# A two-layer hybrid attention backbone: queries and gates projected with features on partitions, and reciprocal sums spread through DRAM

## The chip, the cores and the metric

The kernel runs on one core of one Trainium2 chip. The metric is the device time of one execution in microseconds; the median of three runs before the change is 1154.01 us (1152.91 to 1156.14). All arithmetic is in fp32; where TensorE is to run at its faster fp32r rate, each operand is split into a high part (rounded to fp32r) and a low part (the rest), and a product is made of three matmuls: high x high, high x low, low x high.

## What is computed

Two layers work on 512 latent tokens and 256 context tokens of width 1024. In each layer a modulated RMSNorm feeds one input projection of 4608 columns. These are split among three groups of eight heads (head width 64) and a gate of 1536 columns. Cut to what the change touches:

```python
# A: global attention, q and k normalised per head, rotary on latent tokens
q = apply_rope(rmsnorm(heads(q, 8), qn), cos, sin) * HEAD_DIM ** -0.5
p = softmax(q @ k_all.T);  ya = p @ v_all              # k_all: 512 latent + 256 context keys
# B: 16-column neighbourhood of the 8 x 64 grid, with a learned bias, plus context keys
# C: window of +-128 tokens with a sink logit, rotary, plus context keys
ux = concat([ya, yb, yc]) * silu(px[9])                # the gate
x = x + gate * (ux @ w_out)
```

Context tokens go through the same weights in layer 0 as queries that read context keys alone. In layer 1 only latent queries are needed. So a layer has 6 tiles of 128 query tokens (layer 0) or 4 (layer 1), called `nq`.

## The kernel before

**Stages.** A prologue (L370 to L447) norms x, makes the modulation and accumulates the first projections while it goes. Then `mixers` runs once for each layer, and after each an output projection (L530 on) makes the residual and the next layer's norm, or the result. Inside `mixers` the heads go in pairs: 4 pairs of B, 4 of A, 4 of C, twelve to a layer, in the order of `PLAN` (L34). While pair n attends, the projections of pair n+1 are made: `weave` (L1406) alternates the two generators by their costs. Only the first slot of a layer has no attention in it.

**Two ways to project.** `proj_f` (L295) puts 128 output features on partitions and tokens in columns: the weights are stationary, and the moving operand has 512 latent or 256 context columns. `proj_t` (L316) puts 128 tokens on partitions: the normed activations are stationary and 256 columns of weights move. Either accumulates 24 matmuls (8 slices of the 1024 inputs, three products each) in a PSUM bank and then calls `done`, which empties the bank. Steady banks are `pj` (two), `T` (two, for transposes), `Sbig` (three, scores) and `Obig` (one, head outputs in two halves).

- B's q and k and all of C (with its gates) come from `proj_f`.
- A's k and v, B's v, **A's q with A's gate** (`a_pair`, L863), and **B's gates** (`b_g`, L923) come from `proj_t`.

**A's q before** (`a_pair`, `rope_a`). For each two tiles of tokens, with a head's 64 features side by side in the free dimension, the rotation, the sum of squares and the normalisation run on POOL (pair 0 on DVE), the result is split in high and low, and four fp32r transposes (L879) bring the features to partitions; ACT copies them to Q. The scale of 1/8 and the norm weight lie in the tables made by `tables_a`.

**C's q** (`rope_c`, `c_q`) has features on partitions from the start. ACT copies the bank to `tA`; four DMAs on SP's queue swap quarters of 32 partitions (L958); three POOL operations rotate (L959 to L961); ACT and POOL write the high and low parts (L969, L970).

**Attention.** For each head `scores` puts q k into `Sbig`; DVE takes the negated maximum, ACT the exponential with its sum; SP's DMA moves P to fp32r tiles (`ship`, L1030). `values` turns P by fp32r transposes into T (L1044), ACT and DVE split it (`pt_copy`: `pth` L778, `ptl` L1024), and matmuls with v accumulate in Obig. `o_out` (L1060) adds its halves into the pair's tile `OT`, features on partitions. There is one `OT` and one `u` buffer.

**Finish of a pair** (`finish`, L1314). The reciprocals of the sums are `rec`: 128 tokens by 2 heads by `nq`. They are needed along columns, so POOL multiplies each tile of the gate (A, B) or of ones (C) by its reciprocal (L1339), an fp32 transpose turns each tile (L1347, recorded at L1047), and DVE multiplies OT by it (L1350, L1357). For C, whose gate has features on partitions, POOL multiplies by the gate after that (L1353, L1355). The product `u` is stored to DRAM on ACT's queue (L1365), or, for the last three in `FT_ORDER`, split at once for the output projection. C's last pair of a layer uses `end=True`: one DVE copy spreads the reciprocals (L1335), and DVE does the gate.

**The order.** `arrange` (L1918) sorts all instructions before the program is built. It knows a cost for each kind (`Step.cost`, L1609; for a DMA issue, transfer and landing), the buffers each tag has (`CAPS`) and the dependencies, runs a list scheduler six times with ranks from a backward pass, and fixes the best order of each engine. Engines then run these queues in order.

## Time and profile before

| what | value |
|---|---|
| median of three runs | 1154.01 us (1152.91 to 1156.14) |
| the profiled execution | 1156.11 us, span 1154.3 us |
| TensorE busy, instructions | 1122.4 us (97%), 8016 |
| DVE, ACT, POOL busy | 763.6, 685.9, 405.9 us |
| mean granted TensorE clock | 0.997 |
| DMA | 191.40 MB, 105760 packets |

A row of the timeline is: start, length, engine, line, operation, output and inputs, partitions x elements, and a count where like rows are merged. A matmul's length holds its way through the array, so one begins before the last has ended; the distance of two starts says what it costs. "idle before" names what ended the engine's idle time. A row of the groups is: line, engine, operation, tiles, shape, count, busy us, mean ns, idle time before. Of a DMA, the last number is the median time from issue to landing. A helper's line stands for all its callers: L1044 is every transpose of P, L1047 every transpose of `finish`, L1028 every matmul of attention.

### The profile page before, as it was taken

The page shows a single profiled execution, that of the slowest core. Times are in us where ns is not written, and L with a number is a line of the kernel's source. Part 1 is how long each engine was busy: PE and PEld are TensorE (multiplying, and loading weights), DVE is VectorE, ACT ScalarE, POOL GpSimd, SP SyncE. Part 2 cuts the span into 40 slices and gives each one's busy share as a digit, 9 for nine tenths or more (in the row PEclk, how much of TensorE's full clock was granted, in tenths as well). Part 3 has the DMA queues.
Part 4 walks back from the last instruction along what each step waited for, and adds up shares of the span by engine and source line. Part 5 has one row for each costly group of instructions (what it writes and reads, how often), then busy time and mean ns, then how long its engine had stood idle before and what let it go on. Part 6 is the DMA issues. An engine that isn't in the chain of part 4 may idle for free. (4 is left out here: it accounts for less than half of the span.)

```text
span 1154.3 us, 22566 instructions
## 1 busy us (share of the span) xinstructions
PE 1122.4 (97%) x8016; PEld 1011.9 (88%) x8016; DVE 763.6 (66%) x1500; ACT 685.9 (59%) x1533; POOL 405.9 (35%) x496
## 2 busy tenths in 40 slices
PE   6999999999999999999999999999999999999996
PEld 3799989998898898988787999998998989898886
DVE  5666776576556666667979855667674566667653
ACT  5446555565557667678633633555566777778651
POOL 2440210125446456366300030221235665466001
PEclk9999999999999999999999999999999999999998
DMA  9444534434435545446867543454344454456352
GB/s 352 174 147 156 172 117 161 146 132 169 145 131 173 174 165 187 153 144 194 274 230 264 164 133 100 149 175 156 117 153 133 148 182 145 161 171 219 119 174 73
DMA packets 105760, 191.40 MB, mean 166 GB/s; under 512 B 12208, under 2 KB 30768, under 8 KB 105648
## 3 DMA queue, kind: packets, MB, share of 16 engines
q1 hardware_dynamic: 101616, 181.71, 47.2%
q10 hardware_dynamic: 4032, 8.26, 1.9%
q8 instruction: 63, 1.03, 0.4%
q14 instruction: 49, 0.40, 0.1%
HBM read 109.05 MB, written 11.14 MB: 104 GB/s over the span
## 5 line engine op out<-in xcount | busy, mean ns | idle before, releaser
L1024 DVE TENSOR_TENSOR ptl<-T,pth 128x512 fp32r<-128x512 f32 (+1 forms) x264 | 172.5, 670 | 93.0 <-ACT pth L778 89.5
L778 ACT ACTIVATE pth<-T 128x512 fp32r<-128x512 f32 (+1 forms) x264 | 148.4, 585 | 69.8 <-PE T L1044 65.1
L329 PE MATMUL pj<-wh,hL 128*128 128x256 f32 x896 | 179.7, 285 | 0.8 <-DVE kt L906 0.8
L308 PE MATMUL pj<-hL,wh 128*128 128x512 f32 x544 | 180.2, 398 | 0.3 <-DVE qt L894 0.2
L242 ACT ACTIVATE wh<-ws 128x512 fp32r<-128x512 f32 x192 | 119.3, 630 | 72.0 <-PE pj L308 21.8
L1028 PE MATMUL Sbig<-kt,qt 128*128 128x256 f32 (+1 forms) x864 | 156.8, 305 | 1.4 <-DVE negm L1260 1.3
L329 PEld LDWEIGHTS pj<-wh,hL 128*128 128x128 f32 x896 | 144.2, 190 | 1.6 <-PE Sbig L1028 1.1
L1028 PEld LDWEIGHTS Sbig<-kt,qt 128*128 128x128 f32 x864 | 125.5, 189 | 10.7 <-DVE negm L1260 2.9
L245 POOL TENSOR_TENSOR wl<-ws,wh 128x512 fp32r<-128x512 f32 x76 | 97.9, 1296 | 99.3 <-ACT wh L242 92.7
L329 PE MATMUL pj<-wl,hL 128*128 128x256 f32 x448 | 128.2, 286 | 0.0
L1028 PE MATMUL Obig<-ptl,vt 128*128 128x256 f32 (+2 forms) x432 | 125.7, 308 | 1.1 <-DVE ptl L1024 1.1
L1028 PE MATMUL Obig<-pth,vt 128*128 128x256 f32 (+2 forms) x432 | 126.5, 306 | 0.0
L1044 PEld LDWEIGHTS T<-identr,R 128*128 128x128 f32 x1024 | 105.5, 140 | 20.4 <-DVE ptl L1024 6.6
L1044 PE MATMUL T<-identr,R 128*128 128x128 f32 x1024 | 115.3, 242 | 3.4 <-DVE ptl L1024 2.4
L245 DVE TENSOR_TENSOR wl<-ws,wh 128x512 fp32r<-128x512 f32 x116 | 85.2, 746 | 45.5 <-ACT wh L242 31.0
L308 PEld LDWEIGHTS pj<-hL,wh 128*128 128x128 f32 x544 | 97.7, 188 | 16.4 <-issue 0.9
L308 PE MATMUL pj<-hL,wl 128*128 128x512 f32 x272 | 108.4, 399 | 0.0
L1028 PEld LDWEIGHTS Obig<-pth,vt 128*128 128x128 f32 x432 | 81.4, 188 | 5.6 <-issue 0.9
L1028 PEld LDWEIGHTS Obig<-ptl,vt 128*128 128x128 f32 x432 | 81.3, 188 | 5.4 <-DVE ptl L1024 1.8
L329 PEld LDWEIGHTS pj<-wl,hL 128*128 128x128 f32 x448 | 85.2, 190 | 0.8 <-issue 0.4
L1150 DVE TENSOR_REDUCE negm<-Sbig 128x1 f32<-128x768 f32 x64 | 61.0, 953 | 23.3 <-ACT P L1152 16.0
L356 POOL TENSOR_TENSOR rstd<-rstd,mhalf 128x2 f32<-128x2 f32 (+1 forms) x6 | 5.4, 893 | 192.7 <-DVE rstd L354 192.7
(336 smaller groups left out, 2530.0 us busy)
## 6 DMA issues: line engine op xcount, KB each, us to landing
R<-P SPq DMA_DIRECT2D x216, 256.0 KB, 2.4
ws<-wf_dram SPq DMA_DIRECT2D x72, 256.0 KB, 3.2
ws<-wt_dram SPq DMA_DIRECT2D x72, 256.0 KB, 3.0
ada<-adaw_dram SPq DMA_DIRECT2D x32, 512.0 KB, 5.7
ws<-wo_dram SPq DMA_DIRECT2D x57, 256.0 KB, 3.4
bm<-mskB_dram SPq DMA_DIRECT2D x16, 576.0 KB, 3.8
R<-P SPq DMA_DIRECT2D x64, 128.0 KB, 2.2
dots<-adat_dram SPq DMA_DIRECT2D x16, 256.0 KB, 3.4
```

The source lines that it names most:

```text
L242: nc.scalar.activation(hi, src, AF.Copy)
L245: eng.tensor_sub(lo, src, hi.bitcast(F32))
L308: nc.tensor.matmul(p[:, 0:n], a[:, r, :], cols(b[kt], c0, n), start=(i == 0), stop=(i == 23))
L329: nc.tensor.matmul(p[:, t * 256:(t + 1) * 256], tok(a[kt], t2 + t), b[:, r, :], start=(i == 0), stop=(i == 23))
L356: nc.gpsimd.tensor_tensor(rstd[:, 0:k], rstd[:, 0:k], mhalf[:, 0:k], op=OP.pow)
L778: nc.scalar.activation(out, src, AF.Copy)
L1024: nc.vector.tensor_sub(lo[:, 0:n], T[:, 0:n], hi[:, 0:n].bitcast(F32))
L1028: return nc.tensor.matmul(*args, **kw)
L1044: return nc.tensor.transpose(out.bitcast(F32R), src, identr)
L1150: nc.vector.tensor_reduce(nm, S, axis=AX.X, op=OP.max, negate=True)
```

## The change

1. A's q, A's gates and B's gates are projected by `proj_f`, in blocks of 128 features; the weights are laid out for that on the host. `g_silu` is replaced by `f_gate`, which C had as `c_g`.
2. A's q (`a_q`) is copied out, rotated as C's (`rope`, `split_q`) with tables that hold the norm weight, and not normalised. Its squares are summed over each head's 64 partitions by matmuls: the squares' high and low parts are stationary, `pairs` (two columns of ones and zeros) moves, and the sums of 128 tokens by 2 heads land in q's own bank. `rs` = (sum + 64 EPS)^-0.5 holds 1/8 of the inverse norm; it multiplies the negated maximum on DVE and is the scale of the exponential on ACT.
3. `finish` turns the pair's reciprocals once (12 or 8 columns), writes them to DRAM, and reads each head's row back onto its 64 partitions of `u`, all on ACT's queue. DVE multiplies OT by that, and POOL by the gate, for A, B and C alike. The last C pair of each layer keeps its turned tiles, which now lie in `u`.

```diff
-WT_A_KV, WT_A, WT_BV, WT_BG = 0, 1, 5, 7
-WF_BQ, WF_BK, WF_CQ, WF_CK, WF_CV, WF_CG = 0, 4, 8, 12, 13, 14
+WT_A_KV, WT_BV = 0, 1
+WF_BQ, WF_BK, WF_CQ, WF_CK, WF_CV, WF_CG, WF_AQ, WF_AG, WF_BG = 0, 4, 8, 12, 13, 14, 18, 22, 26
...
+    def tables_q():
+        for c in range(2):
+            t = tabs["q", c] = p1.tile([128, NT], F32, name=f"tabq{c}", bufs=1)
+            nc.sync.dma_start(t, trigQ[c])
+            w = SM_QN + 2 * l + c
+            en("tab").tensor_scalar(t, t, sm[:, w:w + 1], None, op0=OP.mult)
...
+    def a_q(i, bank):
+        q = p1.tile([128, NT], F32, name="tA", bufs=CFG["tA"])
+        r = slot("tR")
+        rs = p1.tile([128, 6, 2], F32, name="rs", bufs=3)
+        def done(p, c0, n):
+            hi, lo = [p1.tile([128, NT], F32R, name="qd", bufs=2)[:, 0:n] for _ in range(2)]
+            sq = p1.tile([128, NT], F32, name="th", bufs=1)[:, 0:n]
+            if c0:
+                nc.scalar.activation(r[:, NT:NA], p, AF.Copy, scale=sm[:, SM_QN + 2 * l:SM_QN + 2 * l + 1])
+                nc.scalar.activation(sq, p, AF.Square)
+            else:
+                nc.scalar.activation(q, p, AF.Copy)
+                nc.vector.tensor_mul(sq, p, q)
+            nc.scalar.activation(hi, sq, AF.Copy)
+            nc.gpsimd.tensor_sub(lo, sq, hi.bitcast(F32))
+            first = None
+            for t in range(n // 128):
+                for x in (hi, lo):
+                    m = nc.tensor.matmul(p[:, 2 * t:2 * t + 2], x[:, t * 128:(t + 1) * 128], pairs, start=first is None,
+                                         stop=x is lo, skip_group_check=True)
...
+            v = rs[:, t0:t0 + k].rearrange("p t h -> p (t h)")
+            nc.vector.tensor_scalar(v, p[:, 0:2 * k], HD * EPS, None, op0=OP.add)
+            nc.gpsimd.tensor_tensor(v, v, mhalf[:, 0:2 * k], op=OP.pow)
+        yield from proj_f(l, WF_AQ + i, need_cq, bank, done)
+        return split_q(rope(q, r, "q")), rs
     def a_pair(i, bank):
...
-        yield from proj_t(l, WT_A + i, nq, bank, done)
-        return Q, G
+        Q, rs = yield from a_q(i, bank)
+        G = yield from f_gate(WF_AG + i, newG(), bank)
+        return Q, G, rs
...
     def b_g(m, bank):
-        yield from proj_t(l, WT_BG + m, nq, bank, done)
+        G = []
+        for x in range(2):
+            G.append((yield from f_gate(WF_BG + 2 * m + x, newG(), bank)))
         return G
...
+                r = self.c["rs"][:, i, self.h:self.h + 1]
+                nc.vector.tensor_mul(nm, nm, r)
                 P = newP()
-                nc.scalar.activation(P, S, AF.Exp, bias=nm, accum_out=self.stat("sums", i))
+                nc.scalar.activation(P, S, AF.Exp, bias=nm, scale=r, accum_out=self.stat("sums", i))
...
-        for t in range(0 if end else nq):
-            src = onesw[:, None, :].to_broadcast([128, 2, 64]) if kind == "C" else R[:, t]
-            en("fin").tensor_mul(R[:, t], src, rec[:, :, t:t + 1].to_broadcast([128, 2, 64]))
-        yield 0
+        else:
+            T = psT()
+            turn(T[0:2 * nq, 0:128], rec.rearrange("p h t -> p (h t)"), ident)
+            yield 0.11
+            rT = p1.tile([12, 128], F32, name="rT", bufs=1)
+            nc.vector.tensor_copy(rT[0:2 * nq], T[0:2 * nq, 0:128])
+            d = dram.tile([2 * nq, 128], F32, name=f"r{l}_{ft}")
+            nc.scalar.dma_start(d, rT[0:2 * nq])
+            for h in range(2):
+                nc.scalar.dma_start(u[64 * h:64 * h + 64, 0:ncol],
+                                    bass.AP(tensor=d.tensor, offset=d.offset + h * ncol, ap=[[0, 64], [1, ncol]]))
         for c0, n in ((0, 4), (4, nq - 4)):
...
+                S = u[:, a:b]
+            nc.vector.scalar_tensor_tensor(OT[:, a:b], OT[:, a:b], 0.5, S, op0=OP.mult, op1=OP.mult)
+            e = nc.vector if end else nc.gpsimd
+            if kind == "C" and c0 == 0:
+                e.tensor_mul(colmajor(u[:, 0:NT]), rowmajor(OT[:, 0:NT]), colmajor(G[:, 0:NT]))
             else:
-                nc.vector.scalar_tensor_tensor(u[:, a:b], OT[:, a:b], 0.5, T[:, 0:b - a], op0=OP.mult, op1=OP.mult)
-            yield n * 0.11
+                e.tensor_mul(u[:, a:b], OT[:, a:b], G[:, a:b])
+            yield n * 0.11 if end else 0
```

The gates of C, its q, A's k and v and B's q, k and v are computed as before.

More of the change, by code (lines that the diff above doesn't have):

```diff
@@ L88, in body @@
     nc.vector.memset(onesw, 1.0)
+    onepair = const.tile([128, 2], F32)
+    nc.vector.memset(onepair, 0.0)
+    for h in range(2):
+        nc.vector.memset(onepair[64 * h:64 * h + 64, h:h + 1], 1.0)
+    pairs = const.tile([128, 2], F32R)
+    nc.vector.tensor_copy(pairs, onepair)
     negsink = const.tile([128, 16], F32)
@@ L827, in done @@
         def done(p, t2):
[L828 removed]
+            r = rope_k(p, t2)
             next(r)
@@ L943, in colmajor, with rope @@
         return ap.rearrange("p (c r) -> p c r", r=8)
+    def rope(q, r, tab):
+        sw = p1.tile([128, NT], F32, name="tB", bufs=CFG["tA"])
+        for b in range(4):
+            nc.sync.dma_start(sw[b * 32:(b + 1) * 32], q[(b ^ 1) * 32:((b ^ 1) + 1) * 32])
+        en("cr0").tensor_mul(r[:, 0:NT], q, tabs[tab, 0])
+        en("cr1").tensor_mul(sw, sw, tabs[tab, 1])
+        en("cr2").tensor_add(r[:, 0:NT], r[:, 0:NT], sw)
+        return r
     def rope_c(s, scale, need_ctx, bank):
@@ L955, in rope_c, with split_q @@
         yield from proj_f(l, s, need_ctx, bank, done)
-        sw = p1.tile([128, NT], F32, name="tB", bufs=CFG["tA"])
-        for b in range(4):
-            nc.sync.dma_start(sw[b * 32:(b + 1) * 32], q[(b ^ 1) * 32:((b ^ 1) + 1) * 32])
-        en("cr0").tensor_mul(r[:, 0:NT], q, tabs["C", 0])
-        en("cr1").tensor_mul(sw, sw, tabs["C", 1])
-        en("cr2").tensor_add(r[:, 0:NT], r[:, 0:NT], sw)
-        return r
-    def c_q(i, bank):
-        r = yield from rope_c(WF_CQ + i, 0.125, need_cq, bank)
+        return rope(q, r, "C")
+    def split_q(r):
         Q = [newQ() for _ in range(2)]
@@ L971, in c_q @@
         return Q
+    def c_q(i, bank):
+        return split_q((yield from rope_c(WF_CQ + i, 0.125, need_cq, bank)))
     def c_kv(bank):
@@ L997, in c_kv, with f_gate @@
         return K, V
-    def c_g(i, bank):
-        G = p1.tile([128, NA], F32, name="gc", tag="bm", bufs=CFG["bm"])
+    def f_gate(s, G, bank):
         def done(p, c0, n):
@@ L1006, in done @@
             nc.vector.scalar_tensor_tensor(G[:, c0:c0 + n], th[:, 0:n], 1.0, p, op0=OP.add, op1=OP.mult)
-        yield from proj_f(l, WF_CG + i, need_cq, bank, done)
+        yield from proj_f(l, s, need_cq, bank, done)
         return G
@@ L1012, in c_pair @@
         Q = yield from c_q(i, bank)
-        G = yield from c_g(i, bank)
-        return Q, G
+        G = yield from f_gate(WF_CG + i, p1.tile([128, NA], F32, name="gc", tag="bm", bufs=CFG["bm"]), bank)
+        return Q, G, None
     def newP():
@@ L1532, in mixers @@
             else:
-                Q, G = made[kind.lower(), i]
+                Q, G, rs = made[kind.lower(), i]
                 K, V = made[kind.lower() + "kv", 0]
-                prev = units(kind, i, Q, K, V, G, bmc if kind == "C" else None)
+                prev = units(kind, i, Q, K, V, G, bmc if kind == "C" else None, rs)
         if pair == ("A", 0):
@@ L1569 @@
             T=CFG["T"], spr=2, nw=1, P=CFG["P"], R5=CFG["R5"], R2=CFG["R2"], qt=CFG["qt"], kt=CFG["kt"], vt=CFG["vt"], gt=CFG["gt"], negm=2,
-            bm=CFG["bm"], sums=2, pth=CFG["pt"], ptl=CFG["pt"], rec=2, ssA=2, qd=2, qs=1, ex=2, xr=3, xn0=8, room=9,
+            bm=CFG["bm"], sums=2, pth=CFG["pt"], ptl=CFG["pt"], rec=2, ssA=2, qd=2, rs=3, ex=2, xr=3, xn0=8, room=9,
             xn1=8, rbl=2)
@@ L1951, in col_index @@
     wf += [3072 + 1024 + i * 128 + r(128) for i in range(4)]
+    wf += [i * 128 + r(128) for i in range(4)]
+    wf += [3072 + i * 128 + r(128) for i in range(4)]
+    wf += [3072 + 512 + i * 128 + r(128) for i in range(4)]
     return wt, wf
@@ L2001 @@
         ada_b.reshape(2, 24, 128).transpose(2, 0, 1).reshape(128, 48),
-        final_norm_w.reshape(8, 128).T], 1)
+        final_norm_w.reshape(8, 128).T,
+        np.stack([np.tile(np.roll(w, j * 32), 2) for w in q_norm_a for j in range(2)], 1)], 1)
     small = np.ascontiguousarray(small)
-    bcast = np.concatenate([q_norm_a.ravel(), k_norm_a.ravel(), sink_c.ravel()])
+    bcast = np.concatenate([k_norm_a.ravel(), sink_c.ravel()])
     rpb = np.zeros((2, RPB + 2 * RPAD), f32)
```

150 lines of the change are left out of this document (56 added, 94 removed).

## The prediction

> **What bounds the kernel now.** I read the page's busy times first, then TensorE's own list of waits, then stretches of its timeline.
>
> ```profile
> PE 1122.4 (97%) x8016; PEld 1011.9 (88%) x8016; DVE 763.6 (66%) x1500; ACT 685.9 (59%) x1533; POOL 405.9 (35%) x496
> PEclk9999999999999999999999999999999999999998
> ```
>
> TensorE (PE) is busy 97% of the span at the full clock; PEld is its own weight loading, and of the other engines DVE comes next with 66%. A busy PE can still be one that matmuls pass slowly, so the list of what PE waited for decides (waiting instruction, releaser: us in total, times, longest):
>
> ```profile
> PE Obig L347 <- DVE sq L343: 11.2, 1, 11.2
> PE T L1044 <- DVE ptl L1024: 2.4, 5, 0.7
> ```
>
> The 11.2 us is the prologue, before the first norm; the change does not touch it. The list goes by size, so each further releaser costs PE 2.4 us or less in all. So behind the prologue PE issues one matmul behind another, and the time is the sum of what its instructions cost from start to start. That price, not the mean duration, is what I need for each kind of instruction. For 256 and 512 columns:
>
> ```profile
> 902.96 0.28 PE L329 MATMUL pj<-wl,hL 128*128 128x256 f32 x1
> ...
> 905.11 0.28 PE L1028 MATMUL Obig<-pth,vt 128*128 128x256 f32 x1
> ```
>
> ```profile
> 870.11 0.63 PE L308 MATMUL pj<-hL,wh 128*128 128x512 f32 x2
> ...
> 871.49 0.28 PE L1028 MATMUL Sbig<-kt,qt 128*128 128x256 f32 x1
> ```
>
> ```profile
> 1117.17 16.32 PE pj L505 x72
> ```
>
> Eighteen 256-wide matmuls lie between the first two starts: 2.15 / 18 = 0.1194 us. Six 512-wide ones take 1.38 / 6 = 0.230 us in the second stretch, and in the chain of waits 72 take 16.32 us, 0.2267 each. Twice 0.1194 is 0.239, so a wide matmul is 0.009 to 0.012 us cheaper than two narrow ones.
>
> **Projections.** Each A pair's q and gate, and each two B gates, are 256 output columns made with tokens on partitions: 24 matmuls of 256 for each of 6 tiles in layer 0 and 4 in layer 1. That is 6 such blocks x 24 x (6 + 4) = 1440 matmuls, 1440 x 0.1194 = 171.9 us. After, 12 blocks of 128 columns with features on partitions each take 24 of 512 in both layers and 24 of 256 in layer 0: 576 x 0.2267 + 288 x 0.1194 = 165.0 us, or 166.9 with 0.230. The gain is 6.9 or 5.0; I take 6.0, since these matmuls will be mixed with attention as in both rows. The weights loaded and split stay the same in number.
>
> The Trainium skill, "TensorE: Matmul & The Clock Gate", section "Wait — 56ns, not 53.3ns?", gives a fixed cost of about 2.5 ns for each matmul beyond N / 2.4 GHz. By that the 576 matmuls saved would be worth 1.4 us, not 6.0, and the sum below 4.6 us smaller; the trace disagrees, since 0.1194 us is 12.7 ns above 256 / 2.4 GHz.
>
> **Turns of q and of the gates.** A's q no longer goes through TensorE to get its features on partitions (L879), and no turned tile of gate times reciprocal is needed except in C's last pair of each layer.
>
> ```profile
> L879 PE MATMUL T<-identr,qd 128*128 128x128 f32 x80 | 9.3, 239 | 0.0
> ...
> L1047 PE MATMUL T<-ident,gt 128*128 128x128 f32 x80 | 12.7, 275 | 0.0
> ...
> L1047 PE MATMUL T<-ident,tR 128*128 128x128 f32 x40 | 6.4, 273 | 0.0
> ```
>
> ```profile
> 1018.50 0.60 PE L1047 MATMUL T<-ident,gt 128*128 128x128 f32 x4
> 1018.86 0.36 PE L329 MATMUL pj<-wl,hL 128*128 128x256 f32 x1
> 1019.06 0.28 PE L1028 MATMUL Obig<-ptl,vt 128*128 128x256 f32 x1
> ```
>
> ```profile
> 1035.58 0.47 PE L879 MATMUL T<-identr,qd 128*128 128x128 f32 x4
> 1035.88 0.69 PE L308 MATMUL pj<-hL,wh 128*128 128x512 f32 x2
> 1036.41 0.40 PE L308 MATMUL pj<-hL,wl 128*128 128x512 f32 x1
> ```
>
> A turn also delays the matmul behind it, so I count up to the start after that and take the ordinary price off. Four fp32 turns: 0.56 - 0.12 = 0.44, or 0.110 each. Four fp32r turns: 0.83 - 2 x 0.23 = 0.37, or 0.0925 each. The two last pairs keep 6 + 4 of the 120 turns of L1047: 110 x 0.110 = 12.1 us go. With 80 x 0.0925 = 7.4 us, 19.5 us leave PE.
>
> **What PE gets in their place.** Twenty-two pairs turn their 12 or 8 reciprocals once: 22 x 0.11 = 2.4 us (a turn's price goes by its 128 moving columns, and I leave it at that). A's q is normalised inside the exponential, and its sums of squares are matmuls with two moving columns, a high and a low part for each tile and pair: 4 x 2 x (6 + 4) = 80. No such fp32r matmul stands in the trace. The nearest rows:
>
> ```profile
> 873.55 0.81 PE L1044 MATMUL T<-identr,R 128*128 128x128 f32 x8
> 874.20 0.47 PE L308 MATMUL pj<-hL,wh 128*128 128x512 f32 x1
> ```
>
> ```profile
> 1137.81 0.79 PE Obig L633 x8
> ```
>
> Eight fp32r turns with weights just as wide take 0.65, or 0.081 each; eight two-column matmuls in fp32 take 0.79, or 0.099 each. A matmul can't give time back, so the bounds are 0 and 80 x 0.099 = 7.9 us; I take 80 x 0.078 = 6.2, just under the turn, which has the same weights and more columns to move. The same page and section states that matmuls never start closer than about 25 ns however narrow; at that price the 80 would cost 2.0 us, and the sum would be 4.2 us larger. No run here shows it yet.
>
> **The sum on PE:** -6.0 - 19.5 + 2.4 + 6.2 = -16.9 us.
>
> **What lies beside PE.** The finish of a pair gets a longer path: reciprocal, turn, copy, a write to DRAM and two reads spread over 64 partitions each, then the product on DVE and, now for A and B too, one by the gate on POOL. These rows price it:
>
> ```profile
> u<-u ACTq DMA_DIRECT2D x9, 256.0 KB, 2.0
> uf<-u SPq DMA_DIRECT2D x9, 256.0 KB, 3.2
> tB<-tA SPq DMA_DIRECT2D x40, 64.0 KB, 2.0
> ```
>
> A write lands after 2.0 us, a read from DRAM after 3.2; with three issues and the copy that is about 6 us more before the product, and some 1.3 us more on POOL after it. What is late next is the single OT buffer, which the next pair's first head must write (L1063):
>
> ```profile
> 1020.64 0.69 DVE L1357 SCALAR_TENSOR_TENSOR u<-OT,T 128x512 f32<-128x512 f32 x1
> ...
> 1034.15 0.59 ACT L1063 ACTIVATE OT<-Obig 64x512 f32<-64x512 f32 x1 [0.17 <-PE Obig L1028]
> ```
>
> ```profile
> 998.63 1.57 POOL L1353 TENSOR_TENSOR u<-OT,gc 128x512 f32<-128x512 f32 x1
> ...
> 1003.42 0.38 ACT L1063 ACTIVATE OT<-Obig 64x256 f32<-64x256 f32 x1
> ```
>
> After an A pair OT lies free for 12.8 us (1021.33 to 1034.15), more than the added 7.3. After a C pair it lies free for only 3.2 us (1000.20 to 1003.42), so six C pairs may hold a head's output some 3 us; that head is an A unit, which writes one half of Obig while the next takes the other, and PE need not stop. If it does, it costs up to 6 x 3 = 18 us. I put it at 0 and keep part of it in the range.
>
> A's q now takes the path that C's q takes already: copy, four DMAs that swap quarters, three POOL products, a split on ACT and POOL.
>
> ```profile
> L969 ACT ACTIVATE qt<-tR x16: 617/733/847, 313.5 to 1058.0; 64x768 fp32r<-64x768 f32 x8, 64x512 fp32r<-64x512 f32 x8
> L970 POOL TENSOR_TENSOR qt<-tR,qt x16: 1278/1566/1855, 314.4 to 1058.8; 64x768 fp32r<-64x768 f32 x8, 64x512 fp32r<-64x512 f32 x8
> L961 POOL TENSOR_TENSOR tR<-tR,tB x10: 1268/1286/1759, 283.7 to 1049.6; 128x512 f32<-128x512 f32 x10
> ```
>
> After the copy that is 2.0 us for the swap, 3 x 1.29 on POOL, 0.73 and 2 x 1.57 for the split: about 10 us. Its cover is the gate's projection, which now follows q: 24 x (0.2267 + 0.1194) = 8.3 us in layer 0, 5.4 in layer 1, and as much again of attention woven in. The eight C pairs live with that, and none of PE's waits above names L970.
>
> The queues: 32 swaps join SP's 40 of the same kind, in front of P's transfers and the weights; 66 issues join ACT's queue. The second of three there waits until the write has landed, and behind it stands L778, the copy of turned P that PE needs. POOL loses the 110 products of L1339 (0.40 us each) and A's old rotation, and gets the new one: about even. DVE gets 72 scalings of the maximum, a small instruction like L1326's 0.2 us, which also lie between scores and exponential; 14 us on an engine 34% free. All this I put at 0, on the cover named.
>
> **The forecast.** The profiled execution took 1156.11 us (span 1154.3 and 1.8 around it), 2.1 above the median of 1154.0. 1156.1 - 16.9 = 1139.2 there, 1137.1 in terms of the median. I say 1137.
>
> **Rivals.** *Half is given back at the q bank.* The bank of q is now freed only after copy, square, split and sum. ACT 0.6, DVE 0.69, ACT 0.63 and POOL 1.29 make 3.2 us and more with the hand-overs, while the 256-wide group in the other of two banks takes 24 x 0.1194 = 2.9. If PE waits 0.75 us at each of the 12 sums, 9 us return: 1146. For it: the chain crosses four engines. Against: woven attention doubles the 2.9.
>
> *A's q comes late.* If the 10 us are covered by the projection alone in layer 1, each pair waits up to 4.6 us there; at 16.9 / 8 = 2.1 us a pair nothing is left, 1154. C's pairs speak against.
>
> *The round trip blocks ACT, and the kernel is slower.* In 22 finishes the reads wait in order on ACT for the write:
>
> ```profile
> DMA to landing us min/median/max: 2.0/2.5/4.1
> ```
>
> That is for L1365, the store of u on the same queue. If ACT stands the 2.5 us and PE loses half, 22 x 1.25 = 27.5 us are lost: 1165. It decides from 16.9 / 22 = 0.77 us a finish. For it: PE's largest waits are for pth and ptl. Against: ACT is 41% idle and the order of its queue is planned with the landings. The Trainium skill, "DMA: Bandwidth & Descriptors", section "Anatomy of one DMA", speaks for this rival: most of a DMA's fixed 2 us is the receipt of the write, and HBM is the heaviest target. The 2.0 to 4.1 us above agree.
>
> **How the numbers follow.** The forecast gets 0.70, half given back 0.14, q late 0.05, ACT blocked 0.11. Alone, the forecast reaches from 1131 (sums at 0) to 1142 (sums at 7.9, projections at 5.0, and some 2 us of waits). The second case lies above that; I end the range at 1151 and begin it at 1130, a microsecond lower for waits that go with the turns, which leaves 2 in 10 outside. A measurement of this kernel tells about 0.3%, 3.5 us, from no change. Faster 0.84, same 0.05, slower 0.11.
>
> **What would show it.** In kinds: the 1440 narrow matmuls become 576 wide and 288 narrow ones, L879 is gone, the fp32 turns of L1047 fall from 120 to 32. PE stays at 97%, its list of waits without a row above 3 us after the prologue, and no row of Q's split. A row for the two-column sums above 1 us means the bank; long waits for pth, the round trip; waits of L1063 on OT with PE behind, the single buffer. The forecast is wrong if the span falls by less than 8 us.

## The result and the profile after

The changed kernel takes 1188.78 us (median of four runs, 1184.9 to 1191.76), the kernel before 1153.8 us beside it (1152.91 to 1156.14). The ratio is 1.0288, 95% interval 1.0266 to 1.0309: the change makes the kernel 2.9% slower, where the prediction had 1137 us. The profiled execution took 1184.9 us, with a span of 1183.1 us, 28.8 us more than that of before. Medians here and below are of the executions within 1.5% of the fastest of the same kernel; of the changed kernels this leaves out one execution of e20 (2708.48 us).

First the page's busy times and granted clock, as shown of before:

```profile
PE 1121.9 (95%) x7352; PEld 977.3 (83%) x7352; DVE 789.7 (67%) x1548; ACT 689.4 (58%) x1466; POOL 409.8 (35%) x364
PEclk9999999999999999999899999999999999999998
```

TensorE has 664 instructions fewer and is busy as long as before (1122.4 us there). Its waits, largest first:

```profile
PE T L1057 <- DMA R<-P: 13.4, 10, 3.2
PE T L1057 <- DVE ptl L1037: 11.8, 15, 1.7
PE Obig L354 <- DVE sq L350: 11.7, 1, 11.7
PE Sbig L1041 <- DVE negm L1219: 3.0, 5, 1.1
```

L1057 (L1044 before) turns the softmax weights P; its group of before and of after:

```profile
L1044 PE MATMUL T<-identr,R 128*128 128x128 f32 x1024 | 115.3, 242 | 3.4 <-DVE ptl L1024 2.4 <-DMA R<-P 0.2 <-DVE OT L1350 0.2
```

```profile
L1057 PE MATMUL T<-identr,R 128*128 128x128 f32 x1024 | 116.4, 245 | 25.7 <-DMA R<-P 13.4 <-DVE ptl L1037 11.8
```

From 3.4 us the idle time before it grew to 25.7: it waits for P to land, or for the copy of the turn before it. Two stretches show where. They hold the A and C slots of layer 0 and of layer 1 (columns: length, TensorE's busy time and matmuls, granted clock, DMA share, GB/s). Before, then after:

```profile
254.00:574.00 320.00, 316.23 (x2370) 1.00 0.50 170
853.00:1147.00 294.00, 289.53 (x1923) 1.00 0.45 149
```

```profile
257.00:596.00 339.00, 317.98 (x2141) 0.98 0.55 174
872.00:1176.00 304.00, 288.98 (x1731) 1.00 0.47 152
```

614 us became 643: the whole of the loss, with 421 matmuls fewer in them. The rest of the span is 540 us in both. The chain of waits of layer 1's stretch says what stands between the matmuls. After (880 to 1120 us; it reaches back to 903 us, and the line is cut by the view itself):

```profile
by line: DMA R<-P 15.3%; PE pj L315 13.9%; PE Obig L1041 8.4%; PE Sbig L1041 7.9%; issue 7.0%; PE T L1057 6.7%; PE pj L512 4.1%; DVE ptl L1037 3.0%; DVE negm L1167 2.9%; PE Sbig L512 2.2%; ACT P L1171 2.1%; DVE negm L1169 2.1%; ACT pth L785
```

The whole way of A's weights is on it: maximum (L1167), its scaling (L1169), exponential (L1171), transfer (R<-P), turn, split. In these 217 us the transfers of P make 36.8 us, A's maximum 6.9, its scaling 4.9, its exponential 5.1. The view of before reaches back to 1058 us only. Followed in the same manner from the last matmul that ended before 1057.9 us, the chain before holds, in the 205 us from 853, 7.9 us of transfers of P, 1.0 of A's maximum and 3.7 of its exponential. So the way was on the chain already, for a small part.

The rows that price the new pieces:

```profile
L1169 DVE TENSOR_TENSOR negm<-negm,rs x64: 142/159/1615, 272.2 to 1091.5; 128x1 f32<-128x1 f32 x64
...
L1169 DVE TENSOR_TENSOR negm<-negm,rs 128x1 f32<-128x1 f32 x64 | 26.7, 417 | 1.1
L1132 DVE TENSOR_TENSOR negm<-negm,rs 128x2 f32<-128x2 f32 x8 | 4.5, 565 | 0.1
...
L1171 ACT ACTIVATE P<-Sbig,negm,rs x64: 960/993/1012, 272.5 to 1091.8; 128x768 f32<-128x768 f32 x64
  DVE negm L1169: 22.8, 21
...
L881 PE MATMUL pj<-pairs,qd x80: 165/250/250, 251.6 to 1045.0; 128*128 128x2 f32 x80
L1060 PE MATMUL T<-ident,rec x22: 270/271/275, 125.9 to 1100.5; 128*12 128x128 f32 x11, 128*8 128x128 f32 x11
L1060 PE MATMUL T<-ident,u x10: 270/272/273, 605.0 to 1125.8; 128*128 128x128 f32 x10
```

and of before, the exponential and what it waited for:

```profile
L1152 ACT ACTIVATE P<-Sbig,negm x64: 870/902/926, 271.8 to 1063.0; 128x768 f32<-128x768 f32 x64
...
  DVE negm L1150: 8.7, 8
```

The scaling of 128 numbers takes 0.159 us as a median, but 0.417 as a mean, and the exponential waits 22.8 us for it instead of 8.7 us for the maximum.

To set what TensorE does apart from what it waits for, I took the start-to-start distances of all matmuls of each trace, and for each line and width the count times the median distance. The sum of these is TensorE's own price; what the distances hold beyond it is the rest: waits, and matmuls that pass more slowly. Price and rest are of one execution, the time is the median of all, so the two sides can differ by some us.

```
one profiled execution, us                     own price   rest    median time
before                                          1074.5      61.5      1153.8
changed                                         1059.6     104.8      1188.8
e1   scaling on ACT                             1061.3      92.1      1172.3
e2   old finish                                 1072.2      84.3      1178.4
e3   no normalisation                           1052.1      85.7      1158.4
e4   another order                              1059.3     109.9      1192.1
e5   scaling on ACT, old finish                 1071.0      81.8      1173.4
e6   no normalisation, old finish               1062.2      66.9      1146.9
e7   before, with a product of the maximum      1074.8      77.0      1174.6
e8   before, with a product by a constant       1073.7      75.2      1168.6
e9   no maximum, no scaling                     1058.5      71.4      1152.1
e10  the same with the old finish               1069.4      60.0      1153.3
e11  trip issued on SP                          1059.6     105.1      1185.0
e12  before, no maximum                         1073.9      62.5      1158.4
e14  no trip                                    1057.1      86.0      1167.6
e16  small reads                                1060.9      95.9      1181.0
e17  reads that nobody waits for                1059.4      97.3      1182.3
e18  before, another order                      1074.8      64.1      1159.2
e20  order planned with measured costs          1060.0     105.5      1182.1
e21  before, exponential with a scale           1074.5      64.2      1158.6
```

So the instructions did get 14.9 us cheaper (16.9 forecast), and the rest grew by 43.3.

### The profile page after: what moved, and what is told of

It is laid out like the page before. It is cut to its first block, busy times and chain, and to the rows that moved or that the text cites. A ratio compares the mean times of both kernels' runs of the same rounds, so it can differ in the third digit from the quotient of the medians.

```text
span 1183.1 us, 21230 instructions
## 1 busy us (share of the span) xinstructions
PE 1121.9 (95%) x7352; PEld 977.3 (83%) x7352; DVE 789.7 (67%) x1548; ACT 689.4 (58%) x1466; POOL 409.8 (35%) x364
## 5 line engine op out<-in xcount | busy, mean ns | idle before, releaser
L315 PE MATMUL pj<-hL,wh 128*128 128x512 f32 x880 | 294.0, 401 | 1.4 <-DVE rs L889 0.9
L785 ACT ACTIVATE pth<-T 128x512 fp32r<-128x512 f32 (+1 forms) x264 | 147.3, 584 | 88.9 <-PE T L1057 75.4
L315 PEld LDWEIGHTS pj<-hL,wh 128*128 128x128 f32 x880 | 159.8, 188 | 30.6 <-issue 2.6
L315 PE MATMUL pj<-hL,wl 128*128 128x512 f32 x440 | 174.8, 398 | 0.0
L1041 PE MATMUL Sbig<-kt,qt 128*128 128x256 f32 (+1 forms) x864 | 154.3, 307 | 6.7 <-DVE negm L1219 3.0
L1057 PEld LDWEIGHTS T<-identr,R 128*128 128x128 f32 x1024 | 105.6, 141 | 50.0 <-DVE ptl L1037 18.9
L1057 PE MATMUL T<-identr,R 128*128 128x128 f32 x1024 | 116.4, 245 | 25.7 <-DMA R<-P 13.4
L315 PE MATMUL pj<-hC,wh 128*128 128x256 f32 x512 | 100.5, 286 | 0.1
L315 PEld LDWEIGHTS pj<-hL,wl 128*128 128x128 f32 x440 | 82.9, 188 | 13.9 <-issue 0.4
L1171 ACT ACTIVATE P<-Sbig,negm,rs 128x768 f32<-128x768 f32 x64 | 63.4, 991 | 37.7 <-DVE negm L1169 22.8
L315 PEld LDWEIGHTS pj<-hC,wh 128*128 128x128 f32 x512 | 82.2, 191 | 1.9 <-issue 0.3
L1167 DVE TENSOR_REDUCE negm<-Sbig 128x1 f32<-128x768 f32 x64 | 61.0, 954 | 33.4 <-ACT P L1171 21.6
L315 PE MATMUL pj<-hC,wl 128*128 128x256 f32 x256 | 73.3, 286 | 0.0
```

The lines of the kernel that those rows point to most:

```text
L315: nc.tensor.matmul(p[:, 0:n], a[:, r, :], cols(b[kt], c0, n), start=(i == 0), stop=(i == 23))
L785: nc.scalar.activation(out, src, AF.Copy)
L1041: return nc.tensor.matmul(*args, **kw)
L1057: return nc.tensor.transpose(out.bitcast(F32R), src, identr)
L1167: nc.vector.tensor_reduce(nm, S, axis=AX.X, op=OP.max, negate=True)
L1171: nc.scalar.activation(P, S, AF.Exp, bias=nm, scale=r, accum_out=self.stat("sums", i))
```

## The experiments

Four theories stood at the start. **The way of A's weights**: scores, maximum, exponential, transfer and turn follow one another for each of 64 tiles, and what was put into that way delays TensorE. **The finish**: the round trip through DRAM costs time of its own. **The sums**: TensorE's 80 two-column matmuls in the q bank do. **The order**: `arrange` found a bad one.

### Each part alone

```diff
 e1_nm_act      (both places of the scaling)
-                nc.vector.tensor_mul(nm, nm, r)
+                nc.scalar.activation(nm, nm, AF.Copy, scale=r)
 e2_old_finish  (every pair as before: no turn of rec, no DRAM)
+            for t in range(nq):
+                nc.gpsimd.tensor_mul(R[:, t], onesw[:, None, :].to_broadcast([128, 2, 64]),
+                                     rec[:, :, t:t + 1].to_broadcast([128, 2, 64]))
...
-            if end:
+            if True:
                 S = psT()
 e3_no_sums     (a_q without squares, sums and rs)
-                nc.vector.tensor_mul(nm, nm, r)
-                nc.scalar.activation(P, S, AF.Exp, bias=nm, scale=r, ...)
+                nc.scalar.activation(P, S, AF.Exp, bias=nm, ...)
 e4_order_after
-turns=6
+turns=4
```

> The changed kernel (1188.8 us), with the scaling of A's negated maximum by rs moved from DVE to ACT; nothing else is edited. DVE theory: that small product has both inputs in SBUF and stands behind POOL's products (row L1169: median 0.16, longest 1.6 us, 26.7 us in all for 64), inside the chain from scores to exponential; off DVE, 15 to 25 us come back: 1164 to 1174. Round-trip theory (the finish through DRAM): no more than 5 us, 1184 to 1190. Order theory (the list scheduler drew a bad order): anything, as in the run with another order.

> The changed kernel with the third part undone: POOL spreads the reciprocals over 64 columns into u for every pair and each tile is turned by PE (110 fp32 turns of 0.110 us more, 22 small ones less: 9.7 us of PE), no DRAM. Round-trip theory: the 43 us of waits go, PE gets 9.7 more: 1155 to 1160. DVE theory: the scaling of the maximum stays, only the product of OT with u leaves the two-input form (about 7 us of DVE): 1185 to 1195.

> The changed kernel without A's normalisation: no squares, no sums on PE, no rs, no scaling of the maximum, a plain exponential (this part of the computation is left out). The 80 narrow matmuls (7.3 us of PE) go in any theory. DVE theory: 7 + 15 to 25 us, 1157 to 1167, the same as moving the scaling to ACT and 7 less. If the chain of squares and sums (bank held, POOL product in between) is what costs, 1145 to 1155, well below the run with the scaling on ACT. Round-trip theory: 1180.

> The changed kernel, same instructions, with the list scheduler stopped after four of its six passes, so that another order of nearly the same planned length is fixed. Order theory: it moves by 10 us or more, in either direction. All other theories: within 5 us of 1188.8.

Measured: e1 1172.33 us (ratio to before 1.0123, 1.0089 to 1.0157), e2 1178.40 (1.0183, 1.0149 to 1.0217), e3 1158.40 (1.0013, 0.9992 to 1.0034), e4 1192.11 (1.0293, 1.0247 to 1.0339).

Another order costs 3 us, so differences of some 4 us between kernels, whose orders are planned anew, tell nothing (e20, below, makes it some 7). e1 and e3 lie where the DVE theory had them; e2 lies between its two forecasts (1155 to 1160, and 1185 to 1195). Each part taken out gives back more than its instructions hold: the finish of before is 10 us faster though TensorE's price rises by 12.6; without the normalisation 30 us go, of which its price is 7.5. One instruction of 0.417 us a tile as a mean, moved from DVE to ACT, where it takes 0.291, is worth 16.5 us. The order alone is ruled out; the rest needs pairs.

### Two parts together, and one part put into the kernel before

```diff
 e5_act_and_old      both edits of e1 and e2
 e6_nosums_and_old   both edits of e3 and e2
 e7_before_tt        (the kernel before)
                 nc.vector.tensor_reduce(nm, S, axis=AX.X, op=OP.max, negate=True)
+                nc.vector.tensor_mul(nm, nm, onesw[:, 0:1])
 e8_before_ts        (the kernel before, same place)
+                nc.vector.tensor_scalar(nm, nm, 1.0, None, op0=OP.mult)
```

> The changed kernel with both edits: A's negated maximum scaled on ACT, and the finish by POOL and PE turns instead of DRAM. Alone they gave 16.5 and 10.4 us. Two separate causes (the scaling in the softmax chain, the finish): the gains add, 1162 +- 4. One shared cause (DVE held by POOL in two-input products, which both edits thin out): less than the sum, 1167 to 1172.

> The changed kernel without A's normalisation (left out: squares, sums, scaling, as before) and with the finish by POOL and PE turns. What is left of the change is the projection with features on partitions, q's rotation as C's, and the gate as a product of its own on POOL. If these parts hold what the sum on PE said of them (6.0 + 7.4 us off PE) the kernel takes 1140 to 1145. If waits remain in them, 1148 to 1158.

> The kernel before, with one instruction more for each of A's 64 latent tiles: DVE multiplies the negated maximum by a column of ones in SBUF (two inputs, 128x1) between maximum and exponential. If A's softmax chain is hidden by PE's other work, as the prediction had it, 1154 to 1157. If the chain sets the pace in A's slots, each costs at least its 0.16 us, 10 us in all, and with waits behind POOL 0.4 us, 26 us: 1164 to 1180.

> The same place and count in the kernel before, but a multiplication by the constant 1.0 (one input, 128x1). Chain theory without POOL's part: as with two inputs, both at 1164 to 1170. If POOL's hold on DVE's second input is the larger part, this one is at least 6 us faster than the two-input form. If hidden: 1154 to 1157.

Measured: e5 1173.35 us (1.0158, 1.014 to 1.0177), e6 1146.92 (0.9936, 0.9911 to 0.9961), e7 1174.62 (1.0181, 1.0159 to 1.0203), e8 1168.60 (1.0119, 1.0101 to 1.0138).

e7 and e8 are the clearest runs of the study. They put nothing into the kernel before but a multiplication by one, between A's maximum and its exponential; TensorE's own price doesn't move (1074.8 and 1073.7 for 1074.5). The groups of DVE, e7 then e8:

```profile
L1151 DVE TENSOR_TENSOR negm<-negm,onesw 128x1 f32<-128x1 f32 x64 | 26.0, 405 | 0.9
```

```profile
L1151 DVE TENSOR_SCALAR negm<-negm 128x1 f32<-128x1 f32 x64 | 9.4, 147 | 0.9
```

64 x 0.147 = 9.4 us of work on an engine that is a third idle cost 1168.6 - 1154.9 = 13.7 us. With a second operand in SBUF the same work means 0.405 us and costs another 6.0. So the link itself costs the larger part, whichever form it has, and the slower form the rest, if those 6.0 are not the order's.

A link is longer than its own instruction. From the end of A's maximum to the start of its exponential, as means of the 64 tiles, 0.45 us pass before, 0.85 in e8, 0.96 in e7 and 0.95 in the changed kernel. In e8 0.147 of the added 0.40 is the multiplication. The rest is the queues: in 41 of the 64 tiles DVE does another instruction first, and in 39 ACT is still at another one when the product is done. In e1 the same stretch is 0.92, so its shortening doesn't explain e1's 16.5 us: e1 also takes 31.2 us of work off DVE. No run adds that work to DVE away from the way, so the length of the way and DVE's time are not parted there. DVE as a whole was not full: in the two stretches above it was busy for 64% of the time before and 66% after.

e6 is faster than before by 0.64%, but it does not normalise A's queries; it lies between its forecasts (1140 to 1145, and 1148 to 1158). e5 shows that the gains don't add: the scaling on ACT alone and the old finish alone gave 16.5 and 10.4 us, both 15.4, just past the 1167 to 1172 of one shared cause. With the old finish the move to ACT is worth 5.0 us only. In TensorE's rest the normalisation and the finish do add: 104.8 to 85.7 without the one, to 84.3 without the other, to 66.9 without both, 5.4 above the kernel before.

### The way shortened, and the trip left out

```diff
 e9_no_max      (A's tiles; the normalisation's other parts stay)
-                nc.vector.tensor_reduce(nm, S, axis=AX.X, op=OP.max, negate=True)
-                nc.vector.tensor_mul(nm, nm, r)
-                nc.scalar.activation(P, S, AF.Exp, bias=nm, scale=r, ...)
+                nc.scalar.activation(P, S, AF.Exp, scale=r, ...)
 e10_no_max_old both edits of e9 and e2
 e11_sp_issue   (the write and the two reads)
-            nc.scalar.dma_start(...)
+            nc.sync.dma_start(...)
 e14_no_trip    (turn, copy, write and reads left out)
-                S = u[:, a:b]
+                S = OT[:, a:b]
```

> The changed kernel with A's maximum, and its scaling with it, left out: the exponential starts from the scores and the reciprocal norm alone (which is made 64 times smaller, by a second operation in an instruction that is there already, so that nothing overflows; the output is not the reference's). Two links, some 1.4 us by their own durations, leave each A latent tile's way from scores to exponential, and 64 x (0.96 + 0.42) = 88 us of busy time leave DVE; TensorE's own instructions are all kept. Theory 1 (the way from A's scores to its turned weights sets the pace of A's slots, and the added link cost the time): TensorE's waits come down to those of before, the time is at least 30 us under the changed kernel's, 1138 to 1155. Rival (what was lost lies in TensorE's own sums and in the finish, and taking out the normalisation helped through its 80 sums): 1170 to 1185.

> The kernel without A's maximum and its scaling, and with the finish as it was before (ones times reciprocal on POOL, turned on TensorE, no way through DRAM; the output is not the reference's, as the maximum is left out). TensorE gets about 10 us of turns back. If the finish through DRAM costs waits of its own, whatever bounds A's slots, this one is 8 to 13 us faster than the kernel without the maximum alone, as it was without the sums of squares. If the finish only cost time through the late way of A's weights, it is 5 to 10 us slower, by its turns.

> The changed kernel with the three transfers of a finish (reciprocals out, two spread reads) issued on SP's queue in place of ACT's; all else is the same. If the 66 issues (1.4 us a finish) on ACT in front of exponentials and copies are what the finish costs, the time falls by 5 to 12 us, to 1177 to 1184. If the length of the round trip or the product on DVE is the cost, it stays within 3 us of 1189; if SP's queue, which carries the turned weights P, then waits for the write to land, it rises by 5 us or more.

> The changed kernel with the round trip left out: no turn of the reciprocals, no copy, no write to DRAM, no spread reads; DVE multiplies OT by itself, so the product has the same shape and two inputs in SBUF, and the product by the gate on POOL stays (the output is not normalised and not the reference's). 22 turns leave TensorE, 2.4 us. If the round trip (its length, or its issues on ACT) is what the finish costs, the time falls by 8 to 14 us, to 1175 to 1181. If the product from SBUF on DVE, next to POOL, is the cost, it falls by no more than 4 us.

Measured: e9 1152.1 us (0.9984, 0.9969 to 1.0), e10 1153.31 (0.9989, 0.997 to 1.0008), e11 1184.95 (1.0265, 1.0247 to 1.0283), e14 1167.58 (1.0124, 1.0101 to 1.0148).

e9 gives 36.7 us back, as the way theory had it (30 or more), with every instruction of TensorE kept, the 80 sums among them. So the sums cost no more than their own price. e9 also frees DVE of 88 us of work, so it doesn't part the way's length from DVE's time either. The largest waits of e9 behind the prologue:

```profile
PE T L1057 <- DMA R<-P: 5.0, 7, 1.6
PE T L1057 <- DVE ptl L1037: 4.8, 7, 1.4
```

e10 lies between its two forecasts. The trip's own waits are still there (rest 71.4 in e9, 60.0 in e10), and they eat just what its turns save on TensorE (10.9 us of price).

e14 falls by 21.2 us, beyond the 8 to 14 that were expected of the trip, so the trip is the finish's cost, and not the product on DVE, which e14 keeps (medians 0.691 and 0.692 us). The waits for P fall from 13.4 us to 1.5:

```profile
PE T L1057 <- DVE ptl L1037: 8.6, 15, 2.5
...
PE T L1057 <- DMA R<-P: 1.5, 3, 0.9
```

e11 takes the 66 issues off ACT and gains 3.8 us, between its forecasts and no more than another order may, with the rest unchanged (105.1 for 104.8): ACT's queue is not what the trip holds up. Yet the waits for P fall there too, so this row alone does not price the trip:

```profile
PE T L1057 <- DMA R<-P: 5.0, 7, 1.3
```

### What of the trip costs, and how near the kernel before stood

```diff
 e12_before_no_max  (the kernel before)
-                nc.vector.tensor_reduce(nm, S, axis=AX.X, op=OP.max, negate=True)
-                nc.scalar.activation(P, S, AF.Exp, bias=nm, ...)
+                nc.scalar.activation(P, S, AF.Exp, scale=1.0 / 64, ...)
 e16_small_reads    (and the product takes these 64 columns for all)
-                nc.scalar.dma_start(u[64 * h:64 * h + 64, 0:ncol], ...)
+                nc.scalar.dma_start(u[64 * h:64 * h + 64, ncol - 64:ncol], ...)
 e17_side_reads     (dd: a tensor in DRAM)
-                nc.scalar.dma_start(u[64 * h:64 * h + 64, 0:ncol], ...)
+                nc.scalar.dma_start(dd[64 * h:64 * h + 64, 0:ncol], ...)
...
-                S = u[:, a:b]
+                S = OT[:, a:b]
```

> The kernel before with A's maximum left out on latent tiles (64 reductions of 0.96 us on DVE, and one link of the way from scores to weights); the exponential scales by a constant 1/64 instead, so that nothing overflows (the output is not the reference's). TensorE's instructions stay. If the way from scores to weights, or DVE's load, already held TensorE in the kernel before, the time falls by 5 to 15 us, to 1140 to 1150. If the kernel before was bound by TensorE's own instructions, as the prediction read it, it stays within 3.5 us of 1154.

> The changed kernel with each spread read cut to 64 columns (16 KB for 192 or 128 KB); the product takes those 64 columns again and again, so the output is wrong in its normalisation. Turn, copy, write, the waits and the number of issues stay, and so does nearly all of the delay. If the load of the reads on the DMA engines is the cost, the time falls by 10 to 18 us, to 1171 to 1179, near the 1168 without the trip; if the delay is, it stays above 1183.

> The changed kernel with the two spread reads sent to a tensor in DRAM that nobody reads, and the product by OT itself in place of the spread reciprocals, so that nothing waits for the reads: the load on the DMA engines is kept (and a little more, as DRAM is written), the delay of OT and u is gone (the output is not normalised and not the reference's). If the load is the cost, it stays above 1182; if the delay is, it falls to 1168 to 1174.

Measured: e12 1158.38 us (1.0038, 1.0019 to 1.0057), e16 1180.98 (1.0217, 1.019 to 1.0244), e17 1182.28 (1.0238, 1.0192 to 1.0284).

Neither of the trip's two halves is all of it. Without the load 7.8 us go and the rest falls by 8.9; without the delay 6.5 go and the rest falls by 7.5; together 16.4 of the 18.8 by which e14's falls. e16 lies between its two forecasts, e17 at the lower end of the load's (above 1182). The parting is rough: both gains are near what an order may do, and in e16 a read lands after 2.56 us instead of 3.87 (medians), so a part of the delay goes with the load. The load shows on the transfers of P. Their landings, worked out from the trace's semaphore events (each transfer's issue, and the increment that completes it), are parted here by whether a spread read was under way:

```
median us from issue to landing of R<-P (count)
               beside a spread read   apart from one
before              -                   2.38 (312)
changed            3.34 (60)            2.33 (252)
e16               2.44 (59)            2.34 (253)
e17               2.99 (55)            2.35 (257)
e14                 -                   2.35 (312)
```

A fifth of P's transfers lands a microsecond later; among those of 256 KB alone it is 3.64 us (43) beside a read and 2.42 (173) apart from one. The spread reads are 22 pairs of 384 or 256 KB, nearly twice what ACT's queue carried. The pages' rows of that queue (packets, MB, share of 16 engines), before and after:

```profile
q10 hardware_dynamic: 4032, 8.26, 1.9%
```

```profile
q10 hardware_dynamic: 7992, 15.58, 4.1%
```

In e16, with small reads, the waits for P fall from the changed kernel's 13.4 us to about a fifth:

```profile
PE T L1057 <- DMA R<-P: 2.9, 4, 1.2
```

e12 answers the other question. With 61 us of maxima taken from DVE and a link from the way, the kernel before got no faster, 3.6 us slower in fact, which is what an order may do. So it was bound by TensorE's instructions, as the prediction read it, and yet one link more cost 14 to 20 us. As far as these runs tell, the way had just about as much time as it needed.

### The order once more

```diff
 e18_order_before   (the kernel before)
-turns=6
+turns=3
 e20_true_costs     (the planner of the changed kernel)
-            self.fixed = 2400.0 if far else 1650.0
+            self.fixed = (3500.0 if out == "u" else 2400.0) if far else 1650.0
...
+                if self.kind == "InstTensorTensor" and not bank and n <= 2:
+                    d = 420.0
+                elif stem(outs[0][0].name).split("_")[0] == "OT" and not bank:
+                    d = 200.0 + 1.37 * n
 e21_before_scale   (the kernel before)
-                nc.scalar.activation(P, S, AF.Exp, bias=nm, ...)
+                nc.scalar.activation(P, S, AF.Exp, bias=nm, scale=onesw[:, 0:1], ...)
```

> The kernel before, with the same instructions in another order (three rounds of planning in place of six; the planner holds it 2.4 us longer). If orders differ little, as they did for the changed kernel (3 us), it stays within 4 us of 1154. If the order is what the added link cost, it is 10 us or more slower.

> The changed kernel with its order planned from measured durations: 0.42 us for the scaling of the maximum (0.15 before), 1.37 ns a column for the product of OT on DVE (1.06), 1.1 us more for the landing of a spread read. The instructions are the same. If the order was bad because these durations were wrong, the time falls by 8 us or more, below 1181. If the added work itself costs the time, in any order, it stays within 5 us of 1189.

> The kernel before with A's exponential scaled by a column of ones, as the changed kernel scales it by its reciprocal norms: 0.09 us more in 64 exponentials, 5.7 us on the way from scores to weights, with nearly the same order. If that way sets the pace of A's slots tile by tile, the time rises by 4 to 7 us, to 1158 to 1161. If there is slack on it, it stays within 2 us of 1154.

Measured: e18 1159.21 us (1.0029, 1.0017 to 1.004), e20 1182.12 (1.0211, 1.0181 to 1.024), e21 1158.63 (1.0018, 1.0 to 1.0035).

An order that the planner holds 2.4 us longer is 0.3% slower on the chip: about one part in five of what e7's link cost. e20's order, made with measured durations, is 6.7 us better, between its two forecasts (below 1181, and 1184 or more) and with the rest unchanged (105.5); most of the loss is not a matter of wrong costs. It is the most that an order alone did here, so of the differences above, e11's 3.8, e17's 6.5 and the 6.0 between e7 and e8 may be the order's. e21 rose by 2 to 3.5 us, under the 4 to 7 forecast, though its time falls in the range that stood beside them; that is inside what an order may do, so it decides nothing.

No form of the changed kernel that computes the reference beat the kernel before; the best was e1, 1.2% slower.

## Why the prediction was wrong

**What bounds the kernel before** was read rightly (e12), but only half of it. "PE issues one matmul behind another" says that no wait could be won; I took it to say also that the ways between the matmuls had room, and no view that I quoted shows room. An idle DVE (34%) is no slack on a way on which each tile passes DVE twice.

**The sum on PE**, -16.9 us, came out at -14.9. By term, count times median for the projections and the summed distances for the narrow kinds: projections -5.1 (forecast -6.0); the finish's turns 10.6 before and 1.4 after, -9.2 (-12.1 + 2.4 = -9.7); q's turns -6.0 (-7.4); the two-column sums +7.3, 0.091 each (+6.2). These make -13.0; the rest of the 14.9 is spread over kinds that did not change. The distances leave out how late the matmul behind a group starts. Counted as the prediction counted, up to the start after that one, the finish's turns come to -9.5 (13.3 before; 3.8 after, of which 2.4 for the reciprocals, as forecast), q's turns to -7.0, and the sums to +9.0, 0.11 each. So the sums were the worst-sized term, above the 7.9 that was to bound them. The prediction's doubt about the 25 ns that the Trainium skill states in "TensorE: Matmul & The Clock Gate" ("Wait — 56ns, not 53.3ns?") was right: behind 20 of the 80 the next start follows after about 0.028 us, but behind the other 60 after 0.10 to 0.11.

**"All this I put at 0, on the cover named"** is the step that failed, in two of its items.

*The 72 scalings.* The prediction saw that they "also lie between scores and exponential" and covered them by DVE's idle share. Idle time of an engine covers work that nobody waits for; here ACT waits (22.8 us behind L1169), then P's transfer, then the turn. The price was off too: 31.2 us on DVE (26.7 + 4.5) for the 14 forecast. Together with the sums the normalisation costs 30 us (e3), 31.5 with the old finish (e2 to e6): 7 to 10 of TensorE's price and 17 to 19 of its rest. Within it e1 shows that a move off DVE returns 16.5 us (5.0 with the old finish), and e8 that the bare link, put into the kernel before, costs 14.

*The finish.* Its length was right: "about 6 us more before the product" is 1.68 for the write and 3.87 for a read, medians. That OT would cover it all was not, as far as e17 tells: with the delay alone taken out, 6.5 us come back. The load of the reads on the DMA engines, some 7.8 us (e16), had no term at all; I priced each DMA by its own landing and never asked whose landing it would put off. The finish as a whole adds 19 to 20.5 us to the rest (11.4 where A's maximum is left out, e9 and e10) and saves 10 to 13 of price: its saving of 9.7 us, the largest of the change, was paid back twice.

*What held.* A's q is not late: the splits' line L982 names no waiter in the trace. The q bank gives TensorE 0.9 us of waits:

```profile
L315 PE MATMUL pj<-hL,wh 128*128 128x512 f32 x880 | 294.0, 401 | 1.4 <-DVE rs L889 0.9 <-DVE qt L907 0.4
```

so the rivals *half is given back at the q bank* and *A's q comes late* both fell.

**The rival that ended on the right side**, the round trip blocking ACT, had the place but not the mechanism: with its issues on SP the rest is the same (e11). The Trainium skill's account of a DMA's fixed cost ("DMA: Bandwidth & Descriptors", "Anatomy of one DMA"), which I cited for it, puts it at about 2 us, on the path of GpSimd's queue; the writes here, on ACT's, land after 1.68 us (median), and no run shows how much of that is the receipt. What the trip did to P it did by load and by delay, in shares that e16 and e17 part only roughly.

**The accounts.** Rest before 61.5; normalisation 17 to 19, finish 19 to 20.5; 66.9 with neither (e6), so 5.4 are left for everything else, A's q and the gates among it, which no run parts further. Price -14.9 and rest +43.3 make 28.4 of the 28.8 us by which the span grew.

Of the signs named beforehand two did tell: PE fell from 97% to 95%, and two rows of waits rose over 3 us after the prologue. The sign of the round trip did not: it was to be long waits for `pth`, and these make 0.5 us (Obig, L785), while the long ones are for P's transfers and for `ptl`.

## What to carry to other kernels

Before a small instruction is called free, ask whether it lies in series on a way that repeats once a tile; then it costs its time and its hand-over at each tile, however idle its engine, and putting such a link (a multiplication by one) into the old kernel measures that in one run. A busy TensorE without waits says that work can't be taken from the other engines with profit; it doesn't say that work can be added there. A new DMA has two prices, its own latency and the lateness of the transfers beside it, and the second is found by parting the old transfers' landings by whether the new one was under way.

## What was not expected of the hardware

**A tiny DVE instruction waits out a whole POOL instruction.** From the changed kernel's timeline, two places (start, length):

```profile
911.97 1.31 POOL L960 TENSOR_TENSOR tB<-tB,tabx 128x512 f32<-128x512 f32 x1
912.25 1.04 DVE L1169 TENSOR_TENSOR negm<-negm,rs 128x1 f32<-128x1 f32 x1
...
965.40 1.58 POOL L1378 TENSOR_TENSOR u<-OT,gc 128x512 f32<-128x512 f32 x1
965.80 1.20 DVE L1169 TENSOR_TENSOR negm<-negm,rs 128x1 f32<-128x1 f32 x1
```

The product of 128 numbers ends with POOL's product, at 913.29 beside 913.28 and at 967.00 beside 966.98. So it is throughout: of the 64, 26 take longer than 0.2 us, and all 26 end within 0.03 us of the end of an instruction of POOL; none of the other 38 lies inside one. It has two operands in SBUF; e8's, with one, never takes over 0.156 us. The product on OT pays the same way now that both of its operands are in SBUF, 0.901 us as a mean where the one from PSUM (T) took 0.686; 15 of the 22 take 0.68 to 0.70, the other seven 0.89 to 2.34:

```profile
L1375 DVE SCALAR_TENSOR_TENSOR OT<-OT,u 128x512 f32<-128x512 f32 x22 | 19.8, 901 | 6.5 <-issue 4.0 <-DMA u<-r 2.4
```

```profile
L1357 DVE SCALAR_TENSOR_TENSOR u<-OT,T 128x512 f32<-128x512 f32 x16 | 11.0, 686 | 0.8 <-PE T L1047 0.3
```

The Trainium skill, "SBUF — State Buffer", section "SBUF: two separate sides", states it: a DVE operation with two inputs in SBUF and a GpSimd operation that reads SBUF take turns at a shared pair of ports, and the one that comes second is blocked for the whole instruction. The trace agrees, with the 26 of 26 above.

**A wait of TensorE can cost twice.** After some of the longer waits its granted clock is halved for a while (not after all: 2.05 us at 137.9 us passed without). The changed kernel's clock and TensorE rows around 578 us, in stretches and in the timeline:

```profile
576.00:578.00 2.00, 0.00 (x0) 0.94 1.02 278
578.00:584.00 6.00, 5.77 (x26) 0.50 0.66 216
584.00:588.00 4.00, 4.00 (x28) 0.92 0.33 118
```

```profile
578.17 1.55 PE L1057 MATMUL T<-identr,R 128*128 128x128 f32 x8 [2.75 <-DMA R<-P]
579.52 2.46 PE L1041 MATMUL Sbig<-kt,qt 128*128 128x256 f32 x8
581.78 0.63 PE L1041 MATMUL Obig<-pth,vt 128*128 128x512 f32 x1
```

Behind a wait of 2.75 us the clock is 0.50 for some 6 us, and eight matmuls of 256 columns start (581.78 - 579.52) / 8 = 0.283 us apart instead of 0.12. It happens four times in the changed kernel before its last microseconds (near 285, 545, 578 and 595 us), while in stretches of 20 us the kernel before shows a clock under 0.995 in its last one only. By the mean clocks

```profile
core 0: 1154.3 us, clock 0.997
```

```profile
core 0: 1183.1 us, clock 0.989
```

1183.1 x 0.011 = 13.0 us of full-speed clock are missing after and 1154.3 x 0.003 = 3.5 before, so up to about 9.5 of the 43 us are matmuls that passed at half speed. This is the larger part of why TensorE's busy time did not fall: 29.3 us of the 43 are idle time (61.2 for 31.9), the other 14 are counted as busy. The Trainium skill, "TensorE: Matmul & The Clock Gate", section "What's actually happening", has two clock states, full and half, switched by how busy the array was in a window of about 3.4 us; the 0.50 here agrees, and the half-speed stretches before the end, 3.4 and 6.8 us long, are one and two such windows.
